# Five unused pads move TensorE's moving operands to other SBUF addresses in a two-layer encoder

## The chip, the cores and the metric

The kernel runs on one core of a Trainium2 chip. The metric is the device time of one execution in microseconds. Before the change it was 2125.69 us, the median of three runs (2125.62 to 2129.74 us).

## The reference, cut to what matters

Two transformer layers act on 256 tokens of 2048 features, all in float32:

```python
def reference(x, ...):
    for i in range(2):
        h = rms_norm(x, attn_norm[i])
        x = x + (even_mixer(h, ...) if i == 0 else odd_mixer(h, ...))   # projections + attention + projection
        x = x + sq_relu_mlp(rms_norm(x, mlp_norm[i]), w_mlp_in[i], w_mlp_out[i])
    return rms_norm(x, final_norm)

def sq_relu_mlp(h, w1, w2):        # w1: 2048 x 8192, w2: 8192 x 2048
    a = relu(h @ w1)
    return (a * a) @ w2
```

The even mixer has 8 neighbourhood heads and 8 dilated heads, the odd one has 16 query heads over 4 key/value heads; each head is 128 wide.

## The kernel before

**Tiles.** Features lie on the 128 partitions, the 256 tokens along the free dimension. A weight matrix is cut into units: one unit gives 128 output features and holds 16 tiles of 128 x 128 (the k-tiles). Every float32 operand is split into two float32r parts, a rounded one and the rest. Activations stand as pairs: `u[:, k, 0, :]` and `u[:, k, 1, :]` are the two parts of k-tile `k`, 256 columns each, side by side, 2048 bytes in all.

**The inner product.** For each k-tile TensorE does two matmuls (line 142 and line 144, function `k_range`). The first holds the weights' rounded part `h` and streams both parts of the activation, 512 columns. The second holds the weights' rest `l` and streams only the first part again, 256 columns. I call these two a *pair*: 768 streamed columns. Each of the two is led by a weight load (LDWEIGHTS, "PEld"). The streamed operand is called the moving operand.

**What is streamed, stage by stage.** `u` (normed activations) for the head projections and for the first matrix of both MLPs; `o` (attention outputs) for the output projections; `hid` (squared-ReLU activations) for the second matrix of the MLPs. By the loops, `u` is streamed in 29 x 16 pairs in layer 0's attention (three further units are done in step with the first loads, lines 463 and 465), 20 x 16 in layer 1's, and 64 x 16 in each MLP: 2832 pairs. `hid` is streamed in two halves per layer, each 16 units of 32 k-tiles: 2048 pairs, of which the last 32 are done in three matmuls of 256 columns (lines 139, 140, 144). `o` is streamed in 2 x 256 pairs. Each half of an MLP is thus 512 pairs on `u` (32 units), then 512 pairs on `hid`.

**The weight stream.** Half a unit (8 k-tiles, 512 KB) is loaded by one DMA on SyncE's queue into a buffer `r` (six of them). ScalarE writes `h` (line 81), VectorE writes `l` (line 82), into five buffers each, two halves ahead of TensorE.

**Other matmuls.** The value projection (`value_pair`, line 264) turns the roles round: `u` is held, the weights `h` and `l` are streamed, 256 columns a matmul, three for each k-tile and token half. Scores (line 288), transposes of the weights of attention (line 313) and values (line 332) are emitted a few steps after their inputs are ready, between the pairs of later units.

**What sets addresses.** All SBUF tiles come from pools, one behind another, in the order in which the pools and the tiles of `const` are declared: `const` (`xs`, `u`, small parameters), `raw`, `whi`, `wlo`, `held_w`, `work`, and above them one pool at a time of a stage: `attn0`, `mlp0`, `attn1`, `mlp1`. In the stage pools `o` or `hid` is the first tile. Nothing in the code reads an address, and the order of instructions is that in which the code emits them.

Of the kernel before, what the change touches and what calls it, by code (L numbers as in the profile page):

```python
# [7 lines left out]
F32 = mybir.dt.float32  # L8
# [6 lines left out]
P = 128  # L15
# [11 lines left out]
HALF = KT // 2  # L27
RAW_BUFS = 6
PART_BUFS = 5
# steps between the stages of a head's attention  # L30
LAGS_0 = (5,4,3)
LAGS_1 = (4,5,3)
LAGS_END = (3,3,2)
# [7 lines left out]
def encoder(ctx: ExitStack, tc: tile.TileContext, a: dict, outT: bass.AP):  # L41
# [8 lines left out]
    acc_ps = ctx.enter_context(tc.tile_pool(name="acc_ps", bufs=3, space=PSUM))  # L50
    aux_ps = ctx.enter_context(tc.tile_pool(name="aux_ps", bufs=1, space=PSUM))

# [1 line left out]
    xs = const.tile([P, KT, T], F32, name="xs")  # L54
    u = const.tile([P, KT, 2, T], F32R, name="u")
    g = const.tile([P, 5, KT], F32, name="g")
    tabs = const.tile([P, 3, TW], F32, name="tabs")
    mask_a = const.tile([P, GRID], F32, name="mask_a")
# [13 lines left out]
    nc.vector.memset(eps, EPS)  # L72

    def warm(func, after):
        # has the function's table loaded ahead of its use
        nc.scalar.activation(warmed, after, func)

    warm(AF.Sqrt, eps)
# [2 lines left out]
        nc.scalar.activation(hi, src, AF.Copy)  # L81
        nc.vector.tensor_sub(lo, src, hi.bitcast(F32))  # L82

# [1 line left out]
    AHEAD = 2  # L85
    pending = []
    loaded = []

    def need(units, held=0):
        # of the first `held` units the last two k-tiles get tiles of their own  # L90
        for i, src in enumerate(units):
            pending.extend([(src[:, :HALF, :], HALF), (src[:, HALF:, :], HALF - 2 if i < held else HALF)])

# [16 lines left out]
    def take_unit():  # L110
        return take_half()[2] + take_half()[2]

# [1 line left out]
    now = [0]  # L114
    tasks = []

# [35 lines left out]
        done(ps)  # L152

    def some_units(done, act):
        # the last k-tiles of the activations become ready late: leave them for the end
        ps = [acc_ps.tile([P, 2 * T], F32, name="acc") for _ in done]
        parts = []
        for i in range(len(done)):
            parts.append(take_unit())
            if act is not u:  # L160
                assert heads_done >= set(range(KT - 2))
            k_range(ps[i], parts[i], act, range(KT - 2))
        if act is not u:
            finish_tasks()
        for i in range(len(done)):
            k_range(ps[i], parts[i], act, range(KT - 2, KT))
            done[i](ps[i])
# [5 lines left out]
        nc.vector.tensor_add(z, ps[:, :T], t)  # L173
        return z

# [1 line left out]
    def gained(k, which):  # L177
        x, gk = xs[:, k, :], g[:, which, k:k + 1]
        if which == 4:
# [14 lines left out]
    norm = {"ready": False, "waiting": []}  # L194

    def finish_norm(last=None, to=None):
        # mean square with tokens on partitions, 1/rms there, and the same along every partition
        ps = aux_ps.tile([P, 512], F32, name="m_ps", bufs=2)
        parts = [ssq] if last is None else [ssq, last]
        for j in range(2):  # L200
            for n, part in enumerate(parts):
                nc.tensor.matmul(ps[:, j:j + 1], part[:, j * P:(j + 1) * P], ones[:, 0:1],
                                 start=n == 0, stop=n == len(parts) - 1)
        r0, v, e = (work.tile([P, 2], F32, name=n, bufs=1) for n in ("r0", "v", "e"))
        nc.scalar.activation(r0, ps[:, :2], AF.Sqrt, bias=eps, scale=1.0 / D)
        nc.vector.tensor_scalar(v, ps[:, :2], 1.0 / D, EPS, op0=ALU.mult, op1=ALU.add)
        nc.vector.reciprocal(r0, r0)
        nc.vector.scalar_tensor_tensor(e, r0, -0.5, r0, op0=ALU.mult, op1=ALU.mult)
        nc.vector.tensor_mul(e, e, v)
        nc.vector.scalar_tensor_tensor(rcol, e, 1.5, r0, op0=ALU.add, op1=ALU.mult)  # L210
        diag = work.tile([P, 2, P], F32, name="diag", bufs=1)
        for j in range(2):
            nc.vector.tensor_scalar(diag[:, j, :], ident, rcol[:, j:j + 1], None, op0=ALU.mult)

        def along():
            out = aux_ps.tile([P, 512], F32, name="m_ps", bufs=2)
            nc.tensor.matmul(out[:, :T], ones, diag.rearrange("p j t -> p (j t)"), start=True, stop=True)
            to(out[:, :T])
        return along
# [13 lines left out]
        later(2, finish_norm(to=to))  # L233
        norm["ready"] = False

# [1 line left out]
    def head_parts(pool, name, bufs, scale, keep):  # L237
        def done(ps):
            z = joined(ps)
# [11 lines left out]
        return done  # L251

    def value_pair(pool, keep):
        # tokens on partitions, two heads at a time
        ps = acc_ps.tile([P, 2, T], F32, name="acc")
        for half in range(2):
            parts = [take_half()[:2] for _ in range(2)]
            for kk in range(HALF):
                k = half * HALF + kk
                h, l = (w.rearrange("p k c -> p (k c)")[:, (kk % 4) * T:(kk % 4 + 1) * T] for w in parts[kk // 4])  # L260
                for j in range(2):
                    js = slice(j * P, (j + 1) * P)
                    for n, (x, y) in enumerate(((0, h), (0, l), (1, h))):
                        nc.tensor.matmul(ps[:, j, :], u[:, k, x, js], y,  # L264
                                         start=k == 0 and j == 0 and n == 0,
                                         stop=k == KT - 1 and n == 2, skip_group_check=True)
                if kk % 2 == 1:
                    tick()
        assert norm["ready"]
        w = pool.tile([P, 2, 2, T], F32R, name="v", bufs=1)  # L270
        for j in range(2):
            nc.scalar.activation(w[:, 0, j, :], ps[:, j, :], AF.Copy, scale=rcol[:, j:j + 1])
            nc.vector.scalar_tensor_tensor(w[:, 1, j, :], ps[:, j, :], rcol[:, j:j + 1],
                                           w[:, 0, j, :].bitcast(F32), op0=ALU.mult, op1=ALU.subtract)
        keep.append(w)

    def attend(pool, o, head, q, k, v, side, biases, lags, sunk=False):
        """q, k, v: lists that hold the operands once their units are done."""
        def scores():
            if not q or not k:  # L280
                later(1, scores)
# [83 lines left out]

    def mlp(layer, which_next):
        with tc.tile_pool(name=f"mlp{layer}", bufs=1) as pool:
            for b in range(2):
                hid = pool.tile([P, 2 * KT, 2, T], F32R, name="hid")

                def hidden(j):
                    def fn(ps):
                        z = joined(ps)
                        nc.vector.scalar_tensor_tensor(z, z, 0.0, z, op0=ALU.max, op1=ALU.mult)  # L374
                        split(hid[:, j, 0, :], hid[:, j, 1, :], z)
                    return fn

                def added(c, final):
                    def fn(ps):
                        if final:  # L380
                            last_added(ps)
                            return
                        z = joined(ps)
                        y = work.tile([P, T], F32, name="y", bufs=1)
                        nc.vector.tensor_mul(y, z, rb2)
                        nc.vector.tensor_add(xs[:, c, :], xs[:, c, :], y)
                        if b == 1:
                            if which_next == 4:
                                squares(c)
                                gained(c, which_next)  # L390
                            else:
                                gained(c, which_next)
                                squares(c)
                    return fn

                if b == 0:
                    some_units([hidden(0), hidden(1)], u)
                    later(2, norm_for_mlp)
                for j in range(2 if b == 0 else 0, 2 * KT):
                    unit(hidden(j), u)  # L400
                for c in range(KT):
                    final = which_next == 4 and b == 1 and c == KT - 1
                    unit(added(c, final), hid, srcs=2, summed=final)

# [1 line left out]
    w0, w1 = a["even_w_in"], a["odd_w_qkv"]  # L406
    for p in range(8):
        base = 2 * p if p < 4 else 24 + 2 * (p - 4)
# [16 lines left out]
    need([a["odd_w_out"][c] for c in range(KT)], 3)  # L425
    mlp_units(1)

# [1 line left out]
    wps = aux_ps.tile([P, 512], F32, name="m_ps", bufs=2)  # L429
    for _ in range(10):  # L430
        nc.tensor.matmul(wps[:, :P], ones, ones, start=True, stop=True)

# [1 line left out]
    STARTERS = 3  # L434
    GROUPS = ((0, 2), (2, 4), (4, 8), (8, 12), (12, 16))
    starters = [[pending.pop(0)[0] for _ in range(2)] for _ in range(STARTERS)]
# [37 lines left out]
        later(1 + gi, some_squares(gi))  # L474
    later(8, norm_for_heads)

# [1 line left out]
    with tc.tile_pool(name="attn0", bufs=1) as pool:  # L478
        o = pool.tile([P, NH, 2, T], F32R, name="o")
        sl = slopes(8)  # L480

# [38 lines left out]
        finish_tasks()  # L520
    mlp(0, 2)

# [1 line left out]
    with tc.tile_pool(name="attn1", bufs=1) as pool:  # L524
        o = pool.tile([P, NH, 2, T], F32R, name="o")
        sl = slopes(16)
        for p in range(2):
# [27 lines left out]

    mlp(1, 4)

# [1 line left out]
    def to(r):  # L559
        for k0, k1 in ((0, 1), (1, 2)) + tuple((k, k + 2) for k in range(2, KT, 2)):  # L560
            ks = slice(k0, k1)
# [70 lines left out]
```

## Time and profile before

| | |
|---|---|
| median of three runs | 2125.69 us (2125.62 to 2129.74) |
| profiled execution, span from the first to the last instruction | 2127.8 us |
| TensorE matmul busy | 2104.8 us (99%) |
| TensorE weight loads busy | 1852.0 us (87%) |
| VectorE busy | 1340.4 us (63%) |
| ScalarE busy | 1035.6 us (49%) |
| HBM read | 381.89 MB, 180 GB/s over the span |

The profile page gives only the span of the profiled execution; what lies around it is not shown separately. The span lies 2.1 us above the median and inside the three runs. "Busy" of TensorE is the union of matmuls whose ends are modelled and overlap, so 99% says that it hardly ever stands still, not that it streams a column in every cycle. How fast it streams is read from the distances between the starts of matmuls. Times of rows are microseconds from the span's start.

### The profile page before, as it was taken

To read this page: it belongs to the slowest core of one execution; us is meant where nothing else is said; L and a number is where in the kernel's file an instruction comes from. 1 tells how busy PE (TensorE), PEld (TensorE's weight loads), DVE (VectorE), ACT (ScalarE), POOL (GpSimd) and SP (SyncE) were. 2 spreads that over 40 slices of the span, in tenths; PEclk is the share of its full clock that TensorE was granted. 3 is DMA by queue.
4 is the path that set the end of the run, shared out by engine and by line. 5 is a ranking of instruction groups with operands and counts; after the bars stand their busy time and mean duration, and the time that the engine had idled before them with its cause. 6 is when DMAs were issued, how large, how long until landed. Compare 5 with 4: busy or idle time off the path is not lost.

```text
span 2127.8 us, 31825 instructions
## 1 busy us (share of the span) xinstructions
PE 2104.8 (99%) x12438; PEld 1852.0 (87%) x12438; DVE 1340.4 (63%) x2088; ACT 1035.6 (49%) x1602; POOL 23.2 (1%) x33
## 2 busy tenths in 40 slices
PE   8999999999999999999999999999999999999997
PEld 6999998888888888888888998888888888888887
DVE  6766676766655556665656877766655556665554
ACT  6555555544444444444445656544444444444442
POOL 2100000000000000000000000000000000000000
PEclk9999999999999999999999999999999999999998
DMA  9754455555555555555555444555555555555552
GB/s 258 180 171 168 168 170 176 190 180 188 187 187 188 188 186 185 187 187 189 188 188 187 148 162 143 188 185 188 185 187 187 188 188 186 187 188 188 188 188 90
DMA packets 108294, 386.06 MB, mean 181 GB/s; under 512 B 12352, under 2 KB 13392, under 8 KB 108144
## 3 DMA queue, kind: packets, MB, share of 16 engines
q1 hardware_dynamic: 106992, 381.73, 53.2%
q0 software_dynamic: 1008, 2.27, 1.5%
q8 instruction: 97, 1.59, 0.3%
q14 instruction: 53, 0.43, 0.1%
q10 hardware_dynamic: 144, 0.04, 0.0%
HBM read 381.89 MB, written 2.10 MB: 180 GB/s over the span
## 4 chain that ended last, share of the span: by engine, by line
PE 96%; DMA 2%; DVE 1%; SPq 0%; ACT 0%; issue 0%; DVEq 0%; ACTq 0%
PE acc L142 58%; PE acc L144 30%; PE acc L264 5%; PE s_ps L288 1%; PE m_ps L332 1%; DMA r<-in_even_w_in 1%; PE p_ps L313 1%; DMA r<-in_even_w_v 1%; DMA xs<-in_xT 0%; ACT h L81 0%; DVE l L82 0%; DVE xs L562 0%; SPq L440 0%; PE acc L140 0%; PE acc L139 0%
## 5 line engine op out<-in xcount | busy, mean ns | idle before, releaser
L82 DVE TENSOR_TENSOR l<-r,h 128x1024 fp32r<-128x1024 f32 (+3 forms) x729 | 880.8, 1209 | 718.4 <-ACT h L81 716.3
L81 ACT ACTIVATE h<-r 128x1024 fp32r<-128x1024 f32 (+3 forms) x729 | 761.5, 1045 | 985.3 <-PE acc L142 646.9
L142 PE MATMUL acc<-u,h 128*128 128x512 f32 x2820 | 1001.0, 397 | 0.0
L144 PE MATMUL acc<-u,l 128*128 128x256 f32 x2820 | 793.8, 281 | 0.0
L142 PE MATMUL acc<-hid,h 128*128 128x512 f32 x2016 | 705.8, 393 | 0.0
L142 PEld LDWEIGHTS acc<-u,h 128*128 128x128 f32 x2820 | 529.7, 188 | 126.9
L144 PE MATMUL acc<-hid,l 128*128 128x256 f32 x2048 | 571.5, 279 | 0.0
L144 PEld LDWEIGHTS acc<-u,l 128*128 128x128 f32 x2820 | 531.7, 189 | 0.2
L142 PEld LDWEIGHTS acc<-hid,h 128*128 128x128 f32 x2016 | 377.7, 187 | 90.3
L144 PEld LDWEIGHTS acc<-hid,l 128*128 128x128 f32 x2048 | 383.7, 187 | 0.0
L142 PE MATMUL acc<-o,h 128*128 128x512 f32 x500 | 176.2, 394 | 1.1 <-DVE z L173 1.1
L144 PE MATMUL acc<-o,l 128*128 128x256 f32 x500 | 139.6, 279 | 0.0
L264 PE MATMUL acc<-h,u 128*128 128x256 f32 x640 | 119.6, 283 | 0.0
L173 DVE TENSOR_TENSOR z<-acc,t 128x256 f32<-128x256 f32 x275 | 114.4, 418 | 2.2 <-ACT t L171 2.1
L142 PEld LDWEIGHTS acc<-o,h 128*128 128x128 f32 x500 | 93.7, 187 | 23.7 <-DVE z L173 1.7
L171 ACT ACTIVATE t<-acc 128x256 f32<-128x256 f32 x275 | 100.5, 366 | 5.5 <-PE acc L144 2.7
L264 PEld LDWEIGHTS acc<-h,u 128*128 128x128 f32 x640 | 100.9, 190 | 0.5
L144 PEld LDWEIGHTS acc<-o,l 128*128 128x128 f32 x500 | 93.7, 187 | 0.0
L264 PE MATMUL acc<-l,u 128*128 128x256 f32 x320 | 90.0, 281 | 0.0
L264 PEld LDWEIGHTS acc<-l,u 128*128 128x128 f32 x320 | 60.9, 190 | 0.1
L374 DVE SCALAR_TENSOR_TENSOR z<-z 128x256 f32<-128x256 f32 x128 | 54.4, 426 | 4.2
L82 DVE TENSOR_TENSOR hid<-z,hid 128x256 fp32r<-128x256 f32 x128 | 53.4, 419 | 1.3 <-ACT hid L81 1.2
(94 smaller groups left out, 859.3 us busy)
## 6 DMA issues: line engine op xcount, KB each, us to landing
r<-in_w_mlp_in SPq DMA_DIRECT2D x256, 512.0 KB, 4.2
r<-in_w_mlp_out SPq DMA_DIRECT2D x256, 512.0 KB, 4.5
r<-in_even_w_in SPq DMA_DIRECT2D x58, 512.0 KB, 3.8
r<-in_odd_w_qkv SPq DMA_DIRECT2D x40, 512.0 KB, 3.7
r<-in_even_w_v SPq DMA_DIRECT2D x32, 512.0 KB, 3.7
r<-in_even_w_out SPq DMA_DIRECT2D x32, 512.0 KB, 3.7
r<-in_odd_w_out SPq DMA_DIRECT2D x32, 512.0 KB, 3.7
r<-in_odd_w_v SPq DMA_DIRECT2D x8, 512.0 KB, 4.2
```

The source lines that it names most:

```text
L81: nc.scalar.activation(hi, src, AF.Copy)
L82: nc.vector.tensor_sub(lo, src, hi.bitcast(F32))
L142: nc.tensor.matmul(ps, h, act[:, k].rearrange("p a t -> p (a t)"), start=start, stop=False)
L144: nc.tensor.matmul(ps[:, :T], l, act[:, k, 0, :], start=False, stop=stop)
L171: nc.scalar.activation(t, ps[:, T:], AF.Copy)
L173: nc.vector.tensor_add(z, ps[:, :T], t)
L264: nc.tensor.matmul(ps[:, j, :], u[:, k, x, js], y, start=k == 0 and j == 0 and n == 0, stop=k == KT - 1 and n == 2, skip_group_check=True)
L288: nc.tensor.matmul(s_ps[:, i, :], qh[:, x, qs], kh[:, y, :], start=n == 0, stop=n == 2)
L313: nc.tensor.transpose(p_ps[:, j, i * P:(i + 1) * P], s[:, i, j * P:(j + 1) * P], ident)
L332: nc.tensor.matmul(o_ps[:, :T], vv[:, x, j, side * P:(side + 1) * P], pt[:, y, j, :], start=n == 0, stop=n == 5)
L374: nc.vector.scalar_tensor_tensor(z, z, 0.0, z, op0=ALU.max, op1=ALU.mult)
```

## The change

Two unused tiles are put into `const`, one before `u` and one behind it, and one unused tile is put at the front of each stage pool. Nothing reads or writes them. No instruction is added, removed or moved on any engine; comments go away.

```diff
     xs = const.tile([P, KT, T], F32, name="xs")
+    const.tile([P, 96], F32, name="gap0")
     u = const.tile([P, KT, 2, T], F32R, name="u")
+    const.tile([P, 160], F32, name="gap1")
     g = const.tile([P, 5, KT], F32, name="g")
...
         with tc.tile_pool(name=f"mlp{layer}", bufs=1) as pool:
+            pool.tile([P, (232, 168)[layer]], F32, name="gap")
             for b in range(2):
...
     with tc.tile_pool(name="attn0", bufs=1) as pool:
+        pool.tile([P, 112], F32, name="gap")
         o = pool.tile([P, NH, 2, T], F32R, name="o")
...
     with tc.tile_pool(name="attn1", bufs=1) as pool:
+        pool.tile([P, 16], F32, name="gap")
         o = pool.tile([P, NH, 2, T], F32R, name="o")
```

`gap0` is 384 bytes on each partition and `gap1` 640, so `u` moves by 384 and all that lies behind it by 1024. The built programs give these byte addresses on a partition (start of the tile), and what is left of them when they are divided by 512, the size of one 128-column weight tile, and by 128:

| tile | before | rest of 512 | rest of 128 | after | rest of 512 | rest of 128 |
|---|---|---|---|---|---|---|
| `u` | 32896 | 128 | 0 | 33280 | 0 | 0 |
| `o`, layer 0 | 158208 | 0 | 0 | 159680 | 448 | 64 |
| `hid`, layer 0 | 158208 | 0 | 0 | 160160 | 416 | 32 |
| `o`, layer 1 | 158208 | 0 | 0 | 159296 | 64 | 64 |
| `hid`, layer 1 | 158208 | 0 | 0 | 159904 | 160 | 32 |
| `h`, first buffer | 99744 | 416 | 32 | 100768 | 416 | 32 |
| `l`, first buffer | 120224 | 416 | 32 | 121248 | 416 | 32 |
| `q`, `k`, layer 0 | 198656 | 0 | 0 | 200128 | 448 | 64 |
| `q`, `k`, layer 1 | 190976 | 0 | 0 | 192064 | 64 | 64 |

The other buffers of `h` and `l` follow at 4096 bytes and have the same rests. A k-tile of `u`, `o` or `hid` is 2048 bytes and one of `h` or `l` 512, so in every k-tile of a stage the operands have the rests of the table.

## Rows read from the trace of the kernel before

**Rows 1.** Page: span, busy time by engine, and the chain that ended last.
```profile
span 2127.8 us, 31825 instructions
PE 2104.8 (99%) x12438; PEld 1852.0 (87%) x12438; DVE 1340.4 (63%) x2088; ACT 1035.6 (49%) x1602; POOL 23.2 (1%) x33
...
PE 96%; DMA 2%; DVE 1%; SPq 0%; ACT 0%; issue 0%; DVEq 0%; ACTq 0%
PE acc L142 58%; PE acc L144 30%; PE acc L264 5%; PE s_ps L288 1%; PE m_ps L332 1%; DMA r<-in_even_w_in 1%; PE p_ps L313 1%; DMA r<-in_even_w_v 1%; DMA xs<-in_xT 0%; ACT h L81 0%; DVE l L82 0%; DVE xs L562 0%; SPq L440 0%; PE acc L140 0%; PE acc L139 0%
```

**Rows 2.** Waits of TensorE: us in total, times, longest.
```profile
PE acc L463 <- ACT h L81: 6.2, 5, 1.8
PE m_ps L217 <- DVE diag L213: 4.8, 2, 3.1
PE acc L142 <- DVE z L173: 1.1, 2, 0.6
```

**Rows 3.** Stages on `u` and on `hid`: engines' busy us, clock, DMA share, GB/s.
```profile
core 0: us, PE busy (x) PEld busy (x) DVE busy (x) ACT busy (x) POOL busy (x), PEclk, DMA share, GB/s
785.00:965.00 180.00, 180.00 (x1021) 156.37 (x1020) 112.66 (x159) 85.77 (x127) 0.00 (x0) 1.00 0.57 187
965.00:1145.00 180.00, 180.00 (x1029) 156.76 (x1029) 110.16 (x148) 84.65 (x115) 0.00 (x0) 1.00 0.57 188
```

**Rows 4.** Groups of matmuls by line and shape: busy us, mean ns of one.
```profile
L142 PE MATMUL acc<-u,h 128*128 128x512 f32 x2820 | 1001.0, 397 | 0.0
L144 PE MATMUL acc<-u,l 128*128 128x256 f32 x2820 | 793.8, 281 | 0.0
L142 PE MATMUL acc<-hid,h 128*128 128x512 f32 x2016 | 705.8, 393 | 0.0
L144 PE MATMUL acc<-hid,l 128*128 128x256 f32 x2048 | 571.5, 279 | 0.0
L142 PE MATMUL acc<-o,h 128*128 128x512 f32 x500 | 176.2, 394 | 1.1 <-DVE z L173 1.1
L144 PE MATMUL acc<-o,l 128*128 128x256 f32 x500 | 139.6, 279 | 0.0
```

**Rows 5.** Timeline of TensorE: first pair of each 512-pair stage (start us, us).
```profile
597.02 0.40 PE L142 MATMUL acc<-hid,h 128*128 128x512 f32 x1
...
776.23 0.40 PE L142 MATMUL acc<-u,h 128*128 128x512 f32 x1
...
957.12 0.40 PE L142 MATMUL acc<-hid,h 128*128 128x512 f32 x1
...
1136.33 0.40 PE L142 MATMUL acc<-u,h 128*128 128x512 f32 x1
```

**Rows 6.** Timeline of TensorE on `u`, layer 1, after transposes; eight pairs between.
```profile
1179.53 0.60 PE L313 MATMUL p_ps<-ident,s 128*128 128x128 f32 x4
...
1180.66 0.39 PE L142 MATMUL acc<-u,h 128*128 128x512 f32 x1
...
1183.44 0.39 PE L142 MATMUL acc<-u,h 128*128 128x512 f32 x1
```

**Rows 7.** The chain in order of time: value projections and scores, 256 columns each.
```profile
237.37 5.61 PE acc L264 x48
242.98 0.71 PE s_ps L288 x6
243.69 4.20 PE acc L264 x36
```

**Rows 8.** Timeline of TensorE, last unit: twelve 256-column matmuls on `hid`.
```profile
2112.80 0.28 PE L139 MATMUL acc<-hid,h 128*128 128x256 f32 x1
...
2114.24 0.28 PE L202 MATMUL m_ps<-ones,ssq 128*128 128x1 f32 x2
```

## The prediction

> **What bounds the kernel now.** I read the page first: TensorE is busy for 2104.8 of 2127.8 us, and the chain that ended last is 96% TensorE, of which the pairs of lines 142 and 144 alone make 88% [rows 1]. Then its waits: in the whole span the longest kinds are 6.2 us at the start, 4.8 us at the final norm and 1.1 us twice at an output projection [rows 2]. None lies inside the long stages. So nobody makes TensorE wait there, and the only thing left that could move the time is how long TensorE takes over a pair.
>
> That is not read from the durations of matmuls, which overlap and have modelled ends, but from starts. In the middle of the kernel one stage of 512 pairs on `hid` starts at 597.02, the next one on `u` at 776.23, the next on `hid` at 957.12, the next on `u` at 1136.33 [rows 5]. Hence 512 pairs take 179.21 us on `hid` (350.0 ns a pair), 180.89 us on `u` (353.3 ns) and again 179.21 us on `hid`. Two stages that do the same instructions in the same shapes differ by 3.28 ns a pair, and the two `hid` stages agree to the hundredth of a microsecond. The granted clock is 1.00 in both, the DMA share 0.57 in both, VectorE and ScalarE are as busy in one as in the other [rows 3]. [...] The groups by line say the same in their way: a matmul on `u` is 3 to 4 ns longer than one on `hid` at 512 columns and 2 ns at 256; `o` lies with `hid` [rows 4].
>
> What differs between `u` on one side and `hid` and `o` on the other is where the moving operand starts: by the table of addresses `u` starts 128 bytes past a multiple of 512, `hid` and `o` on one, while the held weights start at 416 for all. `o` has the same k-tile count as `u`, so the count is not the cause. Address is not all of it either: in layer 1, right after transposes, pairs on `u` run from 1180.66 to 1183.44, eight of them in 2.78 us, 347.5 ns [rows 6], until the next attention matmuls come. So the same addresses can run at more than one level, by how the streams happen to be phased. I have three levels, then: 347.5, 350.0 and 353.3.
>
> **The change, part by part.** It adds no instruction and no wait; DMAs, ScalarE and VectorE have the same work. Were one of those slower at the new addresses, it would not show: in the stages they are busy for 113 and 86 of 180 us and DMA for 0.57 of the time [rows 3]. What can change is the price of a matmul.
>
> *`u`*, 2832 pairs. After the change it starts at rest 0 of 512 and the weights stay at 416: exactly the residues at which `hid` and `o` run now. I take their price: 353.3 to 350.0, 3.28 ns x 2832 = -9.3 us. Bounds: 0 if the higher bits of the address decide, and -16.4 us if `u` lands on the low level of rows 6 for good (5.8 ns x 2832).
>
> *`hid`*, 2016 whole pairs (the 32 in three pieces are left out). It moves to rest 416 in layer 0 and 160 in layer 1, both 32 bytes past a multiple of 128. No pair of before starts there. The nearest row is the value projection: there the weights are streamed, so the moving operand starts at 416, 32 past a multiple of 128. 48 of its matmuls take 5.61 us and 36 take 4.20 us, 116.8 ns for 256 columns, while six scores, whose moving operand starts at a multiple of 512, take 0.71 us, 118.3 ns [rows 7]. 768 columns in three matmuls are thus 350.4 ns there. Splitting a pair into three costs something: twelve matmuls of 256 columns on `hid` take 1.44 us in the last unit, 360.0 ns for 768 columns [rows 8] against 350.0 in two pieces. So at such a start three pieces cost 9.6 ns less than on `hid` today, and two pieces might cost 340.4 (350.0 - 9.6). The held operand was another one there (`u`), so I take only the lowest level that a pair itself has shown, 347.5: 2.5 ns x 2016 = -5.0 us. Bounds: 340.4 gives -19.4 us. On the other side, the alternation on `u` is an end: its two-pair sum is 706.6, and if one of the two is a quick pair of 347.5, the other is 359.1; that is also about the three-piece price of 360.0. Every pair at 360 would be +10.0 ns x 2016 = +20.2 us.
>
> *`o`*, 512 pairs, rest 448 and 64, both 64 past a multiple of 128: no row has a moving operand there. I take 0, with bounds of -1.3 us (347.5) and +5.1 us (360).
>
> *Other matmuls.* The value projection's 960 matmuls keep their moving operand and get the held one at another rest; scores and values, 384, move by the same pads as `o`. The distance between the two prices of rows 7, 1.5 ns, bounds both ways: 1344 x 1.5 = 2.0 us. I take 0. The 48 starting pairs wait for loads [rows 2]: 0.
>
> The sum on the profiled execution: 2127.8 - 9.3 - 5.0 = 2113.5 us of span. The span was 2.1 us over the median of the runs; carried over, the forecast is 2111.4 us.
>
> [...]
>
> **The rivals.**
>
> *Only `u` gains* (chance 0.18). The low residue decides for `u`, while `hid` and `o` stay at 350.0. For it: today's 350.0 is met by two tiles, in stages with other work around them. Against: 32 past 128 is a start that they never had, and rows 7 show it cheaper. Time: 2125.7 - 9.3 = 2116.4.
>
> *A deeper gain* (0.15). `u` on 347.5 and `hid` at 340.4, `o` at 347.5: -16.4 - 19.4 - 1.3 = -37.1, to 2088.6. For it: rows 6 show that `u` can hold the low level; rows 7 and 8. Against: the low level lasted only till other matmuls came in between.
>
> *No change* (0.12). Either the place of the moving operand isn't what makes `u` and `hid` differ, and the pads do nothing: 2125.7. Or `u` gains and the others go to 353.3: -9.3 + 3.3 x 2528 = -1.0, to 2124.7. For it: one set of addresses has two levels, so phase matters. Against: the repetition of 179.21 us.
>
> *Slower* (0.07). `hid` and `o` leave the multiple of 128 bytes, and every one of their matmuls pays for the crooked start: the pair goes to 360. -9.3 + 20.2 + 5.1 = +16.0, to 2141.7. It ends slower when their pairs rise by more than (9.3 + 4.3) / 2528 = 5.4 ns. For it: today's `u`, off the multiple of 512, is the dearest of the three. Against: rows 7, where the start at 416 is cheap.
>
> **How the numbers follow.** The likeliest is the sum, 2111.4, at 0.48; its own range is 2106 to 2118 (`hid` at 345 in the low case; `hid` unmoved and `o` at 353.3 in the high one). A measurement of this kernel can tell a change of about 0.2%, 4.3 us. Faster by more: the first case, "only `u`" and "deeper", 0.81, and a little of the mixed ones: 0.82. The same: 0.10. Slower: 0.08. The range takes in "no change" above and the middle of "deeper" below: 2094 to 2126; outside are the slower case and the far half of the deeper one, 0.15.
>
> **What would show it.** In the profile after, starts of the 512-pair stages: `u` 179.2 us in place of 180.9, and the `hid` stages at or under 178 us. The mean matmul of line 142 on `u` should fall from 397 to 393 or 394 ns. VectorE, ScalarE and DMA rows should stay. I am wrong if `u` stays at 353.3 (then the low bits of the address don't decide), or if `hid` rises above 350.0 (then 32 past 128 is not the cheap start that I read out of the value projection).

## The result, and the profile after

The changed kernel takes 2114.52 us (median of four runs, 2113.1 to 2115.41) against 2125.65 us, a ratio of 0.9938 with a 95% interval of 0.9925 to 0.995. Run again at the end beside the last experiments it took 2113.6 us against 2127.11, a ratio of 0.9936 (0.9923 to 0.9948). So it is faster by 0.6%, 11 to 13.5 us. The forecast was 2111.4 us.

The page of the changed kernel (two lines further down by numbering: line 142 is now 144, 144 is 146), and the groups that answer to [rows 4]:

```profile
span 2112.8 us, 31825 instructions
...
PE 2090.0 (99%) x12438; PEld 1851.4 (88%) x12438; DVE 1339.8 (63%) x2088; ACT 1036.9 (49%) x1602; POOL 21.4 (1%) x33
...
L144 PE MATMUL acc<-u,h 128*128 128x512 f32 x2820 | 993.6, 394 | 0.1
...
L144 PE MATMUL acc<-hid,h 128*128 128x512 f32 x2016 | 699.1, 391 | 0.0
...
L144 PE MATMUL acc<-o,h 128*128 128x512 f32 x500 | 174.3, 392 | 1.1 <-DVE z L175 1.1
```

The span is 15.0 us shorter than in [rows 1], the counts are the same, and VectorE and ScalarE are as busy as before to 1.3 us. The wide matmul is 2 or 3 ns shorter on all three tiles. Where it went is read from the starts of the 512-pair stages, as in [rows 5] (timeline of TensorE, start us and us of one):

```profile
594.33 0.39 PE L144 MATMUL acc<-hid,h 128*128 128x512 f32 x1
...
771.82 0.40 PE L144 MATMUL acc<-u,h 128*128 128x512 f32 x1
...
951.07 0.40 PE L144 MATMUL acc<-hid,h 128*128 128x512 f32 x1
...
1128.57 0.40 PE L144 MATMUL acc<-u,h 128*128 128x512 f32 x1
```

A stage on `hid` takes 177.49 us (346.7 ns a pair) where it took 179.21; the one on `u` takes 179.25 (350.1) where it took 180.89. Over the four `u` stages of the MLPs the trace gives -6.6 us, over the four `hid` stages -6.7 (the last one, which ends in three-piece pairs, went from 179.5 to 177.9), over the two `o` stages -0.84 and -0.88. That is -15.0, the whole difference of the spans; the rest came out even (-0.3 us up to the first matmul on `o`, +0.2 in layer 1's attention).

The value projections went the other way. These rows of the chain are those of an earlier value projection than in [rows 7]; before, its rows too were 5.61 and 4.20 us:

```profile
87.02 5.63 PE acc L266 x48
...
93.37 4.27 PE acc L266 x36
```

84 matmuls in 9.90 us, 117.9 ns each in place of 116.8: 960 of them cost 1.0 us more. (Read from starts alone it is 118.7 in place of 117.6; the difference is the same.)

### The profile page after: what moved, and what is told of

Read it like the earlier page. It is cut to its first block, busy times and chain, and to the rows that moved or that the text cites. A ratio compares the mean times of both kernels' runs of the same rounds, so it can differ in the third digit from the quotient of the medians.

```text
span 2112.8 us, 31825 instructions
## 1 busy us (share of the span) xinstructions
PE 2090.0 (99%) x12438; PEld 1851.4 (88%) x12438; DVE 1339.8 (63%) x2088; ACT 1036.9 (49%) x1602; POOL 21.4 (1%) x33
## 4 chain that ended last, share of the span: by engine, by line
PE 97%; DMA 2%; DVE 1%; SPq 0%; ACT 0%; issue 0%; DVEq 0%; ACTq 0%
PE acc L144 58%; PE acc L146 30%; PE acc L266 5%; DMA r<-in_even_w_in 2%; PE m_ps L334 1%; PE s_ps L290 1%; PE p_ps L315 1%; DVE xs L567 0%; DVE l L84 0%; ACT h L83 0%; PE acc L142 0%; PE acc L141 0%; SPq L443 0%; PE m_ps L219 0%; SPq L446 0%
```

## The experiments

In what follows the *distance* is the start of the moving operand minus the start of the weights, in bytes, its rest of 512. Before, it is 224 on `u` (128 - 416 + 512) and 96 on `hid` and `o`. In the changed kernel it is 96 on `u`, 0 and 256 on `hid`, 32 and 160 on `o`.

**One part alone: `u`.** The kernel before with the two pads in `const`.

```diff
     xs = const.tile([P, KT, T], F32, name="xs")
+    const.tile([P, 96], F32, name="gap0")
     u = const.tile([P, KT, 2, T], F32R, name="u")
+    const.tile([P, 160], F32, name="gap1")
```

Expected: 

> Only the pads round u: u starts at rest 0 of 512, hid and o stay at rest 0. Theory 'start address' (the price of a pair hangs on where the moving operand starts, in the low nine bits): each 512-pair stage on u takes 179.2 us in place of 180.9, the hid stages stay at 179.2; the MLPs gain 6.5 us, and the attention stages gain or lose up to 2 us, so 2117 to 2121 us. Theory 'all that moves' (the pads act through something else, such as the phase in which stages follow each other): the stages on hid change too, or u does not reach 179.2.

Measured: 2122.44 us, ratio 0.9973 (0.9963 to 0.9982). The hand-overs:

```profile
595.18 0.39 PE L144 MATMUL acc<-hid,h 128*128 128x512 f32 x1
...
774.38 0.39 PE L144 MATMUL acc<-u,h 128*128 128x512 f32 x1
...
953.58 0.39 PE L144 MATMUL acc<-hid,h 128*128 128x512 f32 x1
```

`u` 179.20 us, `hid` 179.20 as before. For `u` alone the first theory holds.

**The other part alone: the stage pools.** The kernel before with the four pads at the front of the stage pools and none in `const`; the rests of 512 of `hid` and `o` are those of the changed kernel.

Expected: 

> Only the pads at the front of the stage pools: hid starts at rests 416 and 160, o at 448 and 64, u stays at 128. Theory 'start address': hid stages 177.5 us in place of 179.2 (-1.7 us four times), o stages -0.85 us twice, u stages unchanged at 180.9; -8.5 us together, 2117 us. Together with the kernel with u alone it adds up to the whole change. Theory 'all that moves': the two parts do not add up.

Measured: 2126.55 us, ratio 0.9995 (0.9986 to 1.0004). Hardly any gain, and the two parts, 0.27% and 0.05%, do not make up the whole. The hand-overs show why:

```profile
595.77 0.39 PE L142 MATMUL acc<-hid,h 128*128 128x512 f32 x1
...
776.68 0.39 PE L142 MATMUL acc<-u,h 128*128 128x512 f32 x1
...
957.59 0.40 PE L142 MATMUL acc<-hid,h 128*128 128x512 f32 x1
...
1135.10 0.39 PE L142 MATMUL acc<-u,h 128*128 128x512 f32 x1
```

The first `hid` stage takes 180.91 us, the second 177.51, with the same tile at the same addresses and the same weight buffers. Layer 1 does the same (180.91 us, then 346.7 ns a pair up to its last unit). In the slow stage the starts repeat every three pairs (118, 241, 120, 236, 113 and 232 ns between them, 1060 in all, 353.3 a pair), in the quick one every pair (230 and 117). Both last from the first units to the end of the stage. So at the distances 0 and 256 there are two lasting patterns. My expectation of -8.5 us was wrong, and "start address decides" is not enough.

**The distance or the start.** The kernel before with 128 bytes more behind `u`: `u` stays where it is, the weights move, and all that lies behind them with them, so that `hid` and `o` keep their distance.

```diff
     u = const.tile([P, KT, 2, T], F32R, name="u")
+    const.tile([P, 32], F32, name="gap1")
```

Expected: 

> The kernel before with 128 bytes of pad behind u: u stays at rest 128 of 512, while the weights h and l go from 416 to 32 and hid and o from 0 to 128. The distance from the weights' start to the moving start becomes 96 on u (what hid has before) and stays 96 on hid and o. Theory 'distance' (price by where the moving operand lies against the weights): u stages 179.2 us, hid stages 179.2, o unchanged; about 2119 us. Theory 'moving start alone' (the weights' place has no say): u stages stay at 180.9, hid stages rise to 180.9 and o by 0.85 us each; about +8.4 us, 2134 us.

Measured: 2121.8 us, ratio 0.9971 (0.996 to 0.9981).

```profile
595.07 0.39 PE L143 MATMUL acc<-hid,h 128*128 128x512 f32 x1
...
774.27 0.39 PE L143 MATMUL acc<-u,h 128*128 128x512 f32 x1
...
953.47 0.39 PE L143 MATMUL acc<-hid,h 128*128 128x512 f32 x1
```

179.20 and 179.20 us, the same as with `u` moved, though `u` lies where it lay; and `hid` at rest 128, where `u` cost 180.9, stays at 179.20. So the place of the moving operand by itself does not set the price; where it lies against the weights does. No run shows by what in TensorE the two act on each other.

**Which weights.** By the starts in the trace of the kernel before, the load of `l` goes with the wide matmul on `h` (both at 776.23 us) and the load of the next `h` with the narrow one on `l` (both at 776.46). Here the buffers of `l` move by 128 bytes while those of `h` stay. The pools behind `l` (`held_w`, whose weights serve 12 pairs on `u` and 12 on `o`, and `work`, which TensorE reads only for the norms) move with it; the stage pools get 384 to stay at their rests.

```diff
+    wlo.tile([P, 32], F32, name="gap", bufs=1)
```

Expected: 

> The kernel before with the buffers of l moved by 128 bytes (rest 32), all else at its rests: u 128, hid and o 0, h 416. The distance to l is then 96 on u and 480 on hid; the distance to h stays 224 on u and 96 on hid. l is loaded while the wide matmul on h streams, h while the narrow one on l streams. Theory 'the load under the wide matmul decides' (l): u stages take 179.2 us, hid stages leave 179.2. Theory 'the load under the narrow matmul decides' (h): u stays at 180.9, hid at 179.2. If both count, u and hid both leave their old prices and u is not 179.2.

Measured: 2116.78 us in one run.

```profile
595.45 0.40 PE L144 MATMUL acc<-hid,h 128*128 128x512 f32 x1
...
772.95 0.40 PE L144 MATMUL acc<-u,h 128*128 128x512 f32 x1
...
952.48 0.40 PE L144 MATMUL acc<-hid,h 128*128 128x512 f32 x1
```

`hid` 177.50, `u` 179.53 us (350.6 a pair), in both layers: both leave their old prices, and `u` misses 179.2. Both loads count.

A rival is that not the loads but the writes of ScalarE and VectorE into `h` and `l` get in TensorE's way, since these move with the buffers. The trace of the kernel before speaks against it: if the 512 pairs on `u` from 776.23 are taken two by two, the quarter in which VectorE was busy least (0.14 of the time) cost 353.3 ns a pair, and so did the quarter in which it was busy throughout; but for the first two, at 349.5, no two pairs lay outside 353.0 to 353.5. The same sorting by ScalarE shows no difference either.

**A map of distances.** Three kernels in which `u` and `hid` are slices of slightly larger tiles and start elsewhere in each stage, one run each:

```diff
-                hid = pool.tile([P, 2 * KT, 2, T], F32R, name="hid")
+                hid = pool.tile([P, 2 * KT * 2 * T + 128], F32R, name="hid")
+                w = HID_OFF[2 * layer + b]
+                hid = hid[:, w:w + 2 * KT * 2 * T].rearrange("p (k a t) -> p k a t", k=2 * KT, a=2)
```

Expected of the first: 

> A scan of starts in one kernel: u and hid are slices of slightly larger tiles and start elsewhere in each stage. hid in its four stages at rests 32, 64, 96 and 128 of 512, u in the two MLPs at 160 and 192, in the two attention stages at 128 and 0; weights at 416, o at 0. Theory 'start address, any tile': hid at 128 takes 180.9 us (what u takes there in the kernel before) and u at 160 takes 177.5 (what hid takes there in the changed kernel). Theory 'each tile has its own price': hid at 128 stays near 179.2 and u at 160 near 180.9. If only the rest of 128 counts, hid at 32 equals hid at 160 (177.5) and hid at 128 equals hid at 0 (179.2).

Of the second: 

> Scan of starts, weights at 416. hid in its four stages at rests 224, 256, 288, 320 of 512, u in the MLPs at 352 and 384, in the attention stages at 64 and 448. Call the distance d the moving start minus the weights' start. Theory 'distance, period 512': no price known for these. Theory 'distance, period 256' (the distances 0 and 256 behaved alike so far): hid at 256 (d 352, as 96) takes 179.2 us a stage, at 288 (as 128) 179.75, at 320 (as 160) 177.5; u at 352 (as 192) and 384 (as 224) 180.9 or, in the low state, 177.5.

Of the third: 

> Scan of starts, weights at 416. hid at rests 448, 480, 8 and 16 of 512, u in layer 0 at 416 in both stages, in layer 1 at 160 (attention) and 32 (MLP). Theory 'distance and state': u at 416 (d 0) takes 177.5 or 180.9 us a stage, never 179.2; u at 32 (d 128) takes 179.75 as hid did there. 8 and 16 bytes past d 96: if the price goes by 16-byte or 32-byte steps of the address, 8 stays at 179.2; if each byte counts it leaves it.

Measured, with all other runs, as the length of a 512-pair stage (the second `u` stage of a layer, since the first has three disturbed units):

| distances | us a stage | ns a pair | seen on |
|---|---|---|---|
| 0, 256 | 177.5 or 180.9 | 346.7, 353.3 | `hid`, `u` |
| 32, 288 | 177.5 | 346.7 | `hid`, `u` |
| 64, 320 | 180.9 | 353.3 | `hid` |
| 96, 352 | 179.2 | 350.0 | `u`, `hid` |
| 104, 112 | 180.9 (104; 112 by its units) | 353.3 | `hid` |
| 128, 384 | 179.8 | 351.1 | `hid`, `u` |
| 160, 416 | 177.5 | 346.7 | `hid` |
| 192, 448 | 180.9 | 353.3 | `hid`, `u` |
| 224, 480 | 180.9, once 177.5 (480) | 353.3, 346.7 | `u`, `hid` |

Five of these stages, all from the third kernel (by distances, layer 0: `hid` 32, `u` 0, `hid` 64; layer 1: `hid` 104, `u` 128; the last line of each layer only ends the stage before it):

```profile
591.23 0.40 PE L146 MATMUL acc<-hid,h 128*128 128x512 f32 x1
...
768.73 0.39 PE L146 MATMUL acc<-u,h 128*128 128x512 f32 x1
...
946.23 0.40 PE L146 MATMUL acc<-hid,h 128*128 128x512 f32 x1
...
1127.14 0.39 PE L146 MATMUL acc<-u,h 128*128 128x512 f32 x1
...
1564.81 0.39 PE L146 MATMUL acc<-hid,h 128*128 128x512 f32 x1
...
1745.71 0.40 PE L146 MATMUL acc<-u,h 128*128 128x512 f32 x1
...
1925.46 0.40 PE L146 MATMUL acc<-hid,h 128*128 128x512 f32 x1
```

In this map the price goes by the distance and not by the tile, and wherever both were tried, distances 256 apart gave the same prices, save for the one quick stage at 480: at 224 no stage stayed quick. The steps are finer than 16 bytes: 8 bytes past distance 96 already costs 1.7 us a stage. And my reading of the value projection is refuted: a start 32 past a multiple of 128 is no cheap start by itself (rests 32 and 288 give 179.8, and 416 can run at 180.9).

**A kick.** If what a stage starts with chooses the pattern, a disturbance ahead of it could choose the quick one at the old addresses. Four unused transposes are put ahead of one unit in each MLP stage on `u`:

```diff
+                    if j == (4 if b == 0 else 0):
+                        kick = aux_ps.tile([P, 4, P], F32, name="m_ps", bufs=2)
+                        for i in range(4):
+                            nc.tensor.transpose(kick[:, i, :], ident, ident)
```

Expected: 

> Addresses of the kernel before, with four unused transposes of 128 x 128 ahead of one unit in each of the four MLP stages on u (0.45 us each plus a short stall, 2 us together). In the trace of before, u ran in the low state of 346.7 ns a pair right after transposes till other matmuls came. Theory 'distance and state' (the same addresses have two stable patterns, and what the stage starts with chooses): the u stages take 177.5 to 178 us in place of 180.9, about -11 us with the cost, 2116 us. Theory 'distance alone': u stages stay at 180.9 plus 0.5, about +2 us, 2129 us.

Measured: 2130.21 us, ratio 1.0013 (1.0003 to 1.0022). It fails. In the first `u` stage of a layer the pairs ran at 353.3 from the second one behind the kick; in the second the old alternation was back after four pairs. At distance 224 no disturbance left a quick pattern that lasted (nor did it in [rows 6]).

One thing in this trace was not asked for. In the first `u` stage of both layers the two units *ahead* of the kick, 32 pairs, were quick. Layer 0 with the kick:

```profile
414.98 0.40 PE L142 MATMUL acc<-u,h 128*128 128x512 f32 x1
...
426.08 0.39 PE L142 MATMUL acc<-u,h 128*128 128x512 f32 x1
```

The same 32 pairs of the kernel before:

```profile
415.27 0.40 PE L142 MATMUL acc<-u,h 128*128 128x512 f32 x1
...
426.56 0.40 PE L142 MATMUL acc<-u,h 128*128 128x512 f32 x1
```

They took 11.10 us (347 ns a pair) against 11.29 (353). Up to the first kick TensorE's instructions are the same in both programs, and so are the addresses. So which pattern a stage falls into is not settled by the program and the addresses alone.

**Distances at which only the quick pattern was seen.** The stage pools alone again, but `hid` at 32 in layer 0 and at 160 in layer 1:

```diff
-            pool.tile([P, (232, 168)[layer]], F32, name="gap")
+            pool.tile([P, (112, 16)[layer]], F32, name="gap")
```

Expected: 

> u as before (rest 128, distance 224), o as in the changed kernel, hid at rest 448 in layer 0 (distance 32) and at 64 in layer 1 (distance 160). Theory 'distance and state': at 0 and 256 a stage on hid has two lasting patterns and the one it falls into hangs on what it follows, which is why moving the stage pools alone gained so little; at 32 and 160 only the low one has been seen. So all four hid stages take 177.5 us though they follow the unchanged u: -6.8, with o -1.7, -8.5 us together, 2118 us. Theory 'u must move first' (anything after the old u runs high): the first hid stage of each layer takes 180.9 again, and the gain is about 1 us.

Measured: 2119.95 us, ratio 0.9963 (0.9951 to 0.9976), against 0.9995 with 0 and 256.

```profile
593.73 0.39 PE L142 MATMUL acc<-hid,h 128*128 128x512 f32 x1
...
771.22 0.39 PE L142 MATMUL acc<-u,h 128*128 128x512 f32 x1
...
952.12 0.39 PE L142 MATMUL acc<-hid,h 128*128 128x512 f32 x1
...
1129.62 0.39 PE L142 MATMUL acc<-u,h 128*128 128x512 f32 x1
```

Both `hid` stages take 177.5 us though they follow the unmoved `u` (180.90), and both in layer 1 are quick too. So the parts did not add up because of the distances 0 and 256: there not every stage fell into the same pattern, at 32 and 160 all did. What picks the pattern at 0 and 256 stays open: with the stage pads alone, both `hid` stages of a layer followed 353.3 ns pairs on `u`, and one was slow and one quick.

**A version that beats both.** The changed kernel with `u` and `hid` at distance 32:

```diff
-    const.tile([P, 96], F32, name="gap0")
+    const.tile([P, 80], F32, name="gap0")
...
-    const.tile([P, 160], F32, name="gap1")
+    const.tile([P, 176], F32, name="gap1")
...
-            pool.tile([P, (232, 168)[layer]], F32, name="gap")
+            pool.tile([P, 112], F32, name="gap")
```

Expected: 

> The changed kernel with other pad sizes: u at rest 448 (distance 32), hid at 448 in both layers, o as in the changed kernel. Theory 'distance and state': u stages 177.5 to 178.4 us in place of 179.2 to 180.1 in the changed kernel, hid 177.5: -6.8 us against the changed kernel in the MLPs and about -1 in layer 1's attention, while the value projections hold u at a new place (up to 2 us either way): 2107 us. If u has a second level at distance 32: not under 2113.

Measured: 2105.53 us, ratio 0.9897 (0.9883 to 0.991). All eight MLP stages run at the quick price:

```profile
591.10 0.39 PE L144 MATMUL acc<-hid,h 128*128 128x512 f32 x1
...
768.60 0.39 PE L144 MATMUL acc<-u,h 128*128 128x512 f32 x1
...
946.09 0.39 PE L144 MATMUL acc<-hid,h 128*128 128x512 f32 x1
```

**One step further.** As that, with `u` at distance 0 in layer 0's attention and at 32 afterwards, by slices.

Expected: 

> u and hid as slices of larger tiles: u at rest 416 in layer 0's attention (distance 0; the scan had that stage 2 us shorter) and at 448 (distance 32) in the three later stages, hid at 448, o at 448 and 64. Theory 'distance and state': as all_low, with layer 0's attention about 2 us shorter: 2105 us. If the attention's 2 us in the scan were a matter of chance, equal to all_low.

Measured: 2103.9 us, ratio 0.989 (0.9875 to 0.9905). Its interval overlaps the last one's, so whether it is faster than that is unclear. In that attention stage undisturbed units ran at 346.7 ns a pair in some places and at 353.8 in others, so distance 0 has both prices there too. My reason for it was mistaken in any case, as the last section shows.

**The changed kernel once more.**

Expected: 

> The changed kernel itself, for a comparison on the same chip: 2114 us, ratio 0.994; hid stages 177.5 us, u stages 179.2 and 180.1.

Measured as given above; its stages took 177.49 and 179.24 us again.

## Why the prediction was right, point by point

*What bounds the kernel* held: no wait came or went in the long stages, and the whole gain is in the price of a pair. (The windows of [rows 3] begin 8 to 9 us behind the stages they stand for; cut at the stages' own starts, VectorE is busy for 113.6 and 108.1 us, and the reading stays.)

*`u`*: the price was right (350.0 forecast, 350.1 found, -6.6 us over the MLPs), and `u` alone showed it. The count was not: I multiplied by all 2832 pairs, but the 784 in the attention stages brought nothing. In layer 1 some pairs had run in the low state of [rows 6] before, and at distance 96 only 350.0 was seen: undisturbed pairs there took 351.0 ns on average before and 350.5 after, and the stage as a whole went from 162.9 to 163.1 us. In layer 0 the 768 value projections took back 0.8 of 1.5 us, and the stretch from the last starting matmul to the first one on `o` shows no gain (287.81 us before, 288.08 after, both with the clock drop of the last section). So -6.6 in place of -9.3.

*`hid`*: -6.7 us in place of -5.0. The term was mis-sized because I read the low level from rows rounded to 10 ns (eight pairs, 347.5); it is 346.7. Its reason was wrong as well. I took 32 bytes past a multiple of 128 for a cheap start; the map shows that it isn't. `hid` is quick in the changed kernel because at distances 0 and 256 it fell into the quick one of two patterns, and with the old `u` ahead of it its first stage does not. So that the `hid` term came out near is luck: the start it was built on gives 179.8 us a stage at rests 32 and 288, slower than before. Here the rival "only `u` gains" came nearer than its working said: with the stage pads alone the `hid` stages together gained nothing.

*`o`*: I took 0, for want of a row; its distances 32 and 160 gave -1.7 us, just past my lower bound of -1.3, which suffers from the same rounding.

*Other matmuls*: 0 taken, 2.0 bounded, +1.0 found in the value projection.

So -14.3 was forecast and -15.0 measured between the two profiles, from a `u` term too large by 2.7 and `hid` and `o` terms too small by 3.4; the medians gave -11.1 and -13.5. The step from the span to the time was wrong as well. I took off 2.1 us because the profiled span lay that far over the median; but every run listed with its span is 1.9 to 2.0 us longer than it, so the profiled execution was the slowest of the three (2129.74). The span was forecast at 2113.5 and came out at 2112.8, and the time at 2111.4 for 2114.52.

What stays open: why the pattern forms. The price went with the distance, both `u` and `hid` changed when `l` alone moved (179.53 and 177.50 us), distances 256 apart gave the same prices but for one stage, and at 0 and 256 the starts repeat every pair or every three; but no run shows the reads of TensorE themselves, and that the levels come from how the streams are phased, as the prediction has it, was my guess. How much of a pair is lost I can only estimate. Among the starting pairs of the trace before, from 20.90 to 23.46 us, the granted clock is 0.50, and a wide matmul is followed after 427 ns and a narrow one after 213, in the proportion of their 512 and 256 columns: 640 ns a pair. Half of that, 320 ns, is my estimate for a clock of 1.00, if the columns alone set the time and go with the clock; 346.7 to 353.3 were measured there, 27 to 33 ns more.

## What to carry to other kernels

Where TensorE never waits, read its price from starts, stage by stage: two stages with the same instructions at different prices, where the clock, the DMA share and the other engines are alike, can come from addresses, as 179.2 and 180.9 us did here. Compare the moving operand's start with the weights' start, not with a round number, and try several distances, since here neighbouring ones differed by up to 2%. Prefer a distance that gave the quick pattern after every kind of stage, as 32 and 160 did here with 177.5 us: at one that has two patterns, a part of a change measured alone says little about the whole.

## What the runs showed of the hardware that was not expected

Beside the two patterns at one address, there was a drop of the granted clock from 1.00 to 0.50 that came with kernels 2 to 3 us longer and looked like an effect of addresses. Two stretches of the kernel before, columns as in [rows 3], the granted clock third from the end:

```profile
44.00:54.00 10.00, 6.89 (x59) 6.69 (x58) 5.71 (x13) 4.78 (x7) 2.30 (x3) 1.00 0.96 271
54.00:59.00 5.00, 5.00 (x26) 4.83 (x26) 3.07 (x8) 1.36 (x5) 0.00 (x0) 0.66 0.97 195
```

The same stretches of the second profile of the changed kernel:

```profile
44.00:54.00 10.00, 8.69 (x72) 8.44 (x72) 7.59 (x14) 5.51 (x7) 2.30 (x3) 1.00 1.05 295
54.00:59.00 5.00, 5.00 (x36) 4.56 (x35) 4.43 (x11) 3.97 (x8) 0.00 (x0) 1.00 0.81 255
```

In the first 60 us TensorE still waits, in the kernel before 6.2 us for `h` of the first loads and 3.1 us for the first norm; it was busy for 6.89 us of ten in the one and for 8.69 in the other. In the first the granted clock of the next five microseconds is 0.66 (0.85, 0.50, 0.50, 0.50 and 0.94 one by one, which is 3.4 us at 0.50 and the rest at 1.00), and 26 matmuls started there in place of 36. TensorE's busy time ahead of it does not tell the two cases apart: 7.93 us of the same ten came before a drop in the first profile of the changed kernel, and 7.45 before none in the last variant. Of the two profiles of the changed kernel, the first has the drop (2112.8 us of span) and the second has not (2110.2). Matmul by matmul, the first falls 1.5 us further behind while its clock is low, where a value matmul takes 213 ns in place of 117; another 0.8 us is a longer wait for the norm just ahead of it.

The third scan, whose short attention stage led me to the last variant, had no such drop; the first two had one. The four profiles without it reach the first matmul on `o` at 320.0 to 320.4 us, with `u` at distances 0, 96 and 224; the ten with it at 321.2 to 323.4. So that stage's 2 us was the drop and the wait ahead of it, and not the distance.
